# Hybrid attention and gMLP block, f32, one core: the opening runs four column blocks side by side instead of three, projection pairs change places, and four PSUM roles of the merge stage are dealt out anew

## The chip, the cores and the metric

The kernel runs on one core of one Trainium2 chip. The metric is the device time of one execution in microseconds (us). Time before: median 1210.89 us of 3 runs (1210.16 to 1210.99).

## The reference

The input x is 2048 rows of 1024 in f32. The reference computes

```python
h = _rms(x, g_pre) * (1.0 + scale) + shift          # scale, shift, gate from c @ w_ada
proj = h @ w_in                                     # 1024 -> 4864
q, k, v, z_a, u_b, v_b, z_b, g_logits = jnp.split(proj, SPLIT_IDX, axis=-1)
y_a = _swa_with_sinks(_rope(q), _rope(k), v, sinks) * silu(z_a)
y_b = gelu(u_b) * spatial_gating(layernorm(gelu(v_b))) * silu(z_b)
merged = sigmoid(g_a) * (y_a @ w_proj_a) + sigmoid(g_b) * (y_b @ w_proj_b)
out = x + gate * _rms(merged @ w_out, g_post)
```

Attention is over a window of 128 with 8 query heads and 2 key heads; the spatial gating works in chunks of 128 rows. The product h @ w_in is most of the work.

## The kernel before, in words

**Products.** A big product is done in seven products instead of eight by Winograd's form of Strassen's scheme. A *block* is 256 output columns by 1024 rows, cut into 2 by 2 quadrants ("11", "12", "21", "22": first the column half `ft`, then the row half). The seven products p = 0 to 6 use seven weight sums (A11, S1, S2, A12, S3, S4, A22) and seven sums of the activations, T[0] to T[6]. Each f32 operand is split into a high part (rounded to f32r by a cast on ACT) and a low part (the remainder, a subtraction on DVE), and `mm3` issues high x high, high x low, low x high. One block and one product are a **step**: 12 matmuls of 128x512 on TensorE (PE). In the order that `mm3` issues them, the second matmul of a step needs the low part of T, and the third the low part of W.

**Weights.** `want(n)` prepares W of step n: load, sums, high cast on ACT, low part on DVE, usually three steps ahead (LA = 3), with four W buffers. The sums of a *fresh* pair are done on DVE for the first NFIRST pairs and on GpSimd (POOL) for the later ones (`combos`). Raw loads go through SP's DMA queue and eight `raw` buffers.

**Results.** A block's products accumulate in PSUM banks with roles X, W, Y, Z (`BANK` says which product goes to which). Between products ACT copies Y<-X and Z<-Y inside PSUM, and `evac` takes the quadrants out at p = 3 ("11"), 4 ("22"), 5 ("12") and 6 ("21").

**Order.** For each half of the rows (s = 0, 1) there are 19 blocks. `slot[0]` counts steps, and `later(n, f)` places work n steps on, ahead of the step's matmuls or (post) behind them; "mid" is halfway. So the program is one fixed order on each engine, and an engine that waits holds up all that stands behind it in its queue. In the opening (s = 0) the first three blocks run product by product: p = 0 for blocks 0, 1, 2, then p = 1, and so on, 21 steps in all, with banks X/W, Y/Z and the two halves of the scores' tile S. Meanwhile T[0] to T[6] are made by `t_part` (scaling, differences and low parts on DVE, high parts on ACT). After the first product comes `second_half`: the norm of the second half of the rows (`rstd` L644, `rstd_out` L653), the other half of the conditioning matmuls (`ada_row` L681), T[1]. Then `second_rows`: `ada_fin` L693, T[2]. From step 21 on one block at a time runs in banks X, W, Y, Z. Two more banks (`bank()`, tile name b) serve small matmuls: transposes, the conditioning, attention's outputs.

**Work beside the blocks** that the change moves: the rotary embedding of k and q (`rope_finish`: `turn` loads a rotated copy, `mix` L888 multiplies on DVE and on POOL, `both` L157 adds on DVE and casts the high part on ACT L892, `low` subtracts on DVE), the layernorm steps (`ln_step`: transposes L859, statistics L863, normalization L871 on DVE), setup of the spatial gating. In the blocks of z_a each evacuation adds a multiplication on DVE (L952).

**Merge stage.** After both halves, four `Pair` blocks do both projections of one half of the rows: each step does the "a" part in banks X, Y, Z, W (`BK`) and then the "b" part in four others: two halves c[0], c[1] of the scores' tile S, and two `bank()` tiles c[2], c[3]. A step's quadrants are gated on DVE (`gated`, L1239) and added on POOL.

Of the kernel before, what the change touches and what calls it, by code (L numbers as in the profile page):

```python
# [26 lines left out]
SM = 0.125  # L27
# [23 lines left out]
NFIRST = 3  # L51
# [4 lines left out]
def hybrid_block(ctx: ExitStack, tc: tile.TileContext, xt, x, wada, wgate, wI, wP, wO,  # L56
# [488 lines left out]
    x_load(1)  # L545

# [128 lines left out]
    def ada_row(hf, kks):  # L675

        if hf not in rows:
            rows[hf] = bank()
# [10 lines left out]
    def ada_fin(hf):  # L689

        o = bank()
# [82 lines left out]
    cur["cap"] = 8  # L774
# [134 lines left out]
    def ev_kv(s):  # L909
        def ev(key, src, psum):  # L910
            h = half(key)
            if ft(key) == 0:
# [4 lines left out]
                rope_finish(h, rope_in(src, psum, "e"), put_out, (7, 4)[h] if s == 0 else h)  # L917
            else:
# [16 lines left out]
                later(2, turn, True)  # L935
# [310 lines left out]
    def run_all():  # L1246
        nonlocal T

        for s in range(NS):
            uz = [{} for _ in range(4)]  # L1250
            kinds = [lambda: ev_vb(s, 0), lambda: ev_vb(s, 2), lambda: ev_kv(s), lambda: ev_q(s, 0), lambda: ev_g(s, 0),
# [36 lines left out]
            if s == 0:  # L1288
                n0 = NFIRST
                S = pS.tile([P, 2, 512], F32, tag="s", name=nm("s"))  # L1290
                bks = [two_banks(BK["X"], BK["W"]), two_banks(BK["Y"], BK["Z"]), two_banks(S[:, 0, :], S[:, 1, :])]
                blks = [Block(bks[i], kinds[i](), "mme"[i]) for i in range(NFIRST)]
                def second_half():
                    rstd(1, BK["Z"])
                    ada_row(1, range(2))
                    rstd_out(1, BK["W"])
                    sum_to(2 * NFIRST + 2)
# [10 lines left out]
                def second_rows():  # L1308
# [231 lines left out]
```

## Time and profile before

| what | value |
|---|---|
| median of 3 runs | 1210.89 us |
| the profiled execution's own time | 1210.93 us |
| its span, first to last instruction | 1209.2 us |
| mean granted TensorE clock | 0.997 |
| PE busy | 1191.1 us, 98% of the span |
| DVE busy | 864.4 us, 71% |
| ACT busy | 631.7 us, 52% |
| POOL busy | 355.2 us, 29% |
| DMA, mean | 258 GB/s |

How to read it: the timeline has an instruction's start, its duration, engine, line, operation, what it writes and reads, and in brackets the idle time of its engine just before it with what ended that. Successive instructions of one kind are merged, "x12" is their count. The ends of matmuls are modelled and overlap the next by a little, so the length of a step is read from start to start. The stretches table gives the busy time of each engine and the count of its instructions within a piece of the span. "W<-raw,W" on DVE is the low part of a weight operand, "T<-x,AS,T" of an activation operand.

### The profile page before, as it was taken

Reading aid. Unit: us, or ns where it says so; the run is one execution under the profiler, and the core shown is the slowest. Engines: PE = TensorE matmul, PEld = TensorE weight load, DVE = VectorE, ACT = ScalarE, POOL = GpSimd, SP = SyncE. Lnnn points to the kernel's source line nnn. Section 1 sums busy time; section 2 is a strip of 40 time slices with the busy share of each in tenths; the row PEclk is TensorE's granted clock in tenths of the full one; section 3 lists DMA queues with packets and bytes.
Section 4 is the critical chain, followed back from the end, with each engine's and each line's share of the span. In section 5 each row is a group of like instructions: output and inputs, shape, how many; then the busy total and the mean of one; then the engine's idle time right before and its main releaser. Section 6 shows DMA issues by size and latency. Waiting matters only on the chain.

```text
span 1209.2 us, 17368 instructions
## 1 busy us (share of the span) xinstructions
PE 1191.1 (98%) x5450; PEld 948.9 (78%) x5450; DVE 864.4 (71%) x1315; ACT 631.7 (52%) x1367; POOL 355.2 (29%) x294
## 2 busy tenths in 40 slices
PE   9999999999999999999999999999999999999997
PEld 3567887887777777888888787777778888888886
DVE  6996889668867667358766776564886867767775
ACT  3575455576756676434345675455844512444443
POOL 0002654323366201013302222311133411155443
PEclk9999999999999999999999999999999999999999
DMA  9635997867999998578789899989967988845452
GB/s 356 225 133 190 319 336 268 253 172 199 300 348 331 315 308 295 185 222 296 259 271 284 248 259 325 280 263 294 336 213 272 383 269 267 294 150 183 131 183 87
DMA packets 227828, 311.47 MB, mean 258 GB/s; under 512 B 20884, under 2 KB 102932, under 8 KB 227736
## 3 DMA queue, kind: packets, MB, share of 16 engines
q1 hardware_dynamic: 227264, 309.68, 79.1%
q8 instruction: 43, 0.70, 0.2%
q0 software_dynamic: 176, 0.53, 0.1%
q14 instruction: 49, 0.40, 0.1%
q10 hardware_dynamic: 296, 0.16, 0.1%
HBM read 200.51 MB, written 104.53 MB: 252 GB/s over the span
## 4 chain that ended last, share of the span: by engine, by line
PE 89%; DVE 7%; ACT 2%; issue 1%; POOL 0%; DVEq 0%; ACTq 0%; POOLq 0%
PE bankY L168 28%; PE bankX L168 20%; PE bankW L168 12%; PE bankZ L168 12%; PE s L168 4%; PE b L168 3%; PE b L1091 2%; PE s L1041 2%; PE s L1042 1%; DVE W L151 1%; PE b L980 1%; DVE e L157 1%; PE b L1076 1%; DVE T L743 1%; PE b L681 1%
## 5 line engine op out<-in xcount | busy, mean ns | idle before, releaser
L168 PE MATMUL bankY<-T,W 128*128 128x512 f32 x1614 | 392.1, 392 | 0.8 <-ACT bankZ L432 0.6
L168 PEld LDWEIGHTS bankY<-T,W 128*128 128x128 f32 x1614 | 300.7, 188 | 63.7 <-ACT bankZ L432 1.0
L151 DVE TENSOR_TENSOR W<-raw,W 128x512 fp32r<-128x512 f32 x330 | 271.6, 827 | 70.6 <-ACT W L216 70.4
L168 PE MATMUL bankX<-T,W 128*128 128x512 f32 x1134 | 279.1, 394 | 1.8 <-DVE T L743 1.7
L216 ACT CAST W<-raw 128x512 fp32r<-128x512 f32 x330 | 203.7, 618 | 131.5 <-PE b L168 29.8
L168 PEld LDWEIGHTS bankX<-T,W 128*128 128x128 f32 x1134 | 210.1, 188 | 48.2 <-DVE T L743 5.0
L168 PE MATMUL bankW<-T,W 128*128 128x512 f32 x696 | 173.1, 395 | 3.4 <-DVE T L743 2.5
L168 PE MATMUL bankZ<-T,W 128*128 128x512 f32 x696 | 168.7, 391 | 0.0
L168 PEld LDWEIGHTS bankW<-T,W 128*128 128x128 f32 x696 | 128.2, 188 | 35.1 <-DVE T L743 4.7
L168 PEld LDWEIGHTS bankZ<-T,W 128*128 128x128 f32 x696 | 130.0, 188 | 26.8
L154 POOL TENSOR_TENSOR S<-x,x 128x512 f32<-128x512 f32 x28 | 37.8, 1354 | 243.0 <-DMA x<-yb 102.7
L154 POOL TENSOR_TENSOR raw<-raw,raw 128x512 f32<-128x512 f32 x48 | 76.5, 1593 | 98.8 <-DVE W L151 47.0
L154 POOL TENSOR_TENSOR S<-raw,raw 128x512 f32<-128x512 f32 x24 | 37.8, 1575 | 134.3 <-DMA raw<-in_wI 53.6
L151 DVE TENSOR_TENSOR T<-x,T 128x512 fp32r<-128x512 f32 (+1 forms) x105 | 69.6, 708 | 8.5 <-ACT T L384 8.3
L157 DVE TENSOR_TENSOR e<-bankY,e 128x512 f32<-128x512 f32 x44 | 30.4, 690 | 61.1 <-PE bankY L168 61.0
L168 PE MATMUL s<-T,W 128*128 128x512 f32 x282 | 69.4, 390 | 1.4 <-DVE q L1239 1.4
L168 PEld LDWEIGHTS s<-T,W 128*128 128x128 f32 x282 | 52.8, 188 | 12.7 <-DVE q L1239 1.8
L154 POOL TENSOR_TENSOR raw<-S,raw 128x512 f32<-128x512 f32 x24 | 34.9, 1455 | 81.8 <-DVE W L151 73.9
L384 ACT CAST T<-x 128x512 fp32r<-128x512 f32 x100 | 56.0, 619 | 2.3 <-PE s L168 2.1
L1070 ACT ACTIVATE P<-P,rc 128x128 f32<-128x128 f32 x128 | 44.5, 396 | 12.6 <-DVE rc L1066 12.3
L411 ACT COPY e<-bankW 128x512 f32<-128x512 f32 x41 | 24.0, 584 | 45.3 <-PE bankW L168 42.7
L432 ACT COPY bankZ<-bankY 128x512 f32<-128x512 f32 x42 | 24.0, 571 | 44.6 <-PE bankY L168 44.5
(267 smaller groups left out, 1453.8 us busy)
## 6 DMA issues: line engine op xcount, KB each, us to landing
raw<-in_wI SPq DMA_DIRECT2D x128, 256.0 KB, 4.6
raw<-sS SPq DMA_DIRECT2D x92, 256.0 KB, 5.0
g<-e SPq DMA_DIRECT2D x64, 256.0 KB, 4.0
sS<-raw SPq DMA_DIRECT2D x45, 256.0 KB, 4.0
T<-in_wada SPq DMA_DIRECT2D x16, 512.0 KB, 8.3
q<-q SPq DMA_DIRECT2D x64, 128.0 KB, 5.7
q<-k_s SPq DMA_DIRECT2D x64, 128.0 KB, 5.1
raw<-m SPq DMA_DIRECT2D x32, 256.0 KB, 4.5
```

The costliest lines, as they stand in the source:

```text
L151: dve.tensor_tensor(out=o, in0=a, in1=b, op=ALU.subtract)
L154: pool.tensor_tensor(out=o, in0=a, in1=b, op=op)
L157: dve.tensor_tensor(out=o, in0=a, in1=b, op=ALU.add)
L168: pe.matmul(o, w[:, i, sl], t[:, j, kt, :], start=start and kt == kts[0] and n == 0, stop=stop and kt == last and n == 2, skip_group_check ...
L216: act.copy(w[:, 0, :], src)
L384: act.copy(T[p][:, 0, kt, :], rs[kt])
L411: act.copy(self.wsb, b["W"])
L432: act.copy(self.b[to], self.b[of])
L681: pe.matmul(rows[hf][64 * i : 64 * (i + 1), :], cact[:, kk : kk + 1].broadcast_to([P, 64]), adaw[hf][kk // 4][:, kk % 4, i * 512 : (i + 1) ...
L1041: pe.matmul(o, q[:, g, :], k[:, 0, :], start=True, stop=False)
L1070: act.activation(out=st["P", kv][:, g, 0:P], in_=st["P", kv][:, g, 0:P], func=AF.Copy, scale=st["rc", kv][:, g : g + 1])
L1091: pe.matmul(o[own, :], v[:, k, own], st["pv", kv][k], start=k == 1, stop=k == 0)
```

## The change

NFIRST goes from 3 to 4: the opening runs four blocks product by product, 28 steps. The fourth block lives in the two `bank()` banks; its Y/W bank is also the bank of `ada_row(1)` and `ada_fin(1)`, and no other small matmul has a bank until step 28. The fourth block's weight sums move from POOL to DVE. `rstd(1)` stays behind step 2, but the rest of `second_half` moves behind step 3.

The pair of the first gates (`ev_g(s, 0)`) trades places with the first q pair: gates are now block 3, q blocks 4 and 5, for both halves; the weights' columns are laid out to match. What used small banks or loads in the opening is moved: the rotary work of k, the transposes of v, `setup_sgu` (19 to 24), `zero_heads` (22 to 28), `load_rope` (18 to 23), and the layernorm steps of the first half, from every three steps (22 + 3i) to five in two (27 + 5i // 2).

In the merge stage c[0], c[1] (the tile S) were X and Y of the "b" part and are now X and W; the two `bank()` tiles were Z and W and are now Y and Z.

```diff
-NFIRST = 3
+NFIRST = 4
...
-        plan = [(0, "A11", "raw"), (1, "A21", "raw"), (1, "A22", ("P", "P", "S")[n] if first else "raw"),
+        plan = [(0, "A11", "raw"), (1, "A21", "raw"), (1, "A22", ("P", "P", "x", "x")[n] if first else "raw"),
...
-                rope_finish(h, rope_in(src, psum, "e"), put_out, (7, 4)[h] if s == 0 else h)
+                rope_finish(h, rope_in(src, psum, "e"), put_out, (9, 3)[h] if s == 0 else h)
...
-                later(2, turn, True)
+                later((3, 10)[h] if s == 0 else 2, turn, True)
...
-            kinds = [lambda: ev_vb(s, 0), lambda: ev_vb(s, 2), lambda: ev_kv(s), lambda: ev_q(s, 0), lambda: ev_g(s, 0),
+            kinds = [lambda: ev_vb(s, 0), lambda: ev_vb(s, 2), lambda: ev_kv(s), lambda: ev_g(s, 0), lambda: ev_q(s, 0),
...
-                later((22, 17)[s] + 3 * i, lambda i=i: ln_step(s, i))
+                later((27 + 5 * i // 2, 17 + 3 * i)[s], lambda i=i: ln_step(s, i))
...
-                bks = [two_banks(BK["X"], BK["W"]), two_banks(BK["Y"], BK["Z"]), two_banks(S[:, 0, :], S[:, 1, :])]
-                blks = [Block(bks[i], kinds[i](), "mme"[i]) for i in range(NFIRST)]
+                bX = bank()
+                rows["bank"] = bank()
+                bks = [two_banks(BK["X"], BK["W"]), two_banks(BK["Y"], BK["Z"]), two_banks(S[:, 0, :], S[:, 1, :]),
+                       two_banks(bX, rows["bank"])]
+                blks = [Block(bks[i], kinds[i](), "mmee"[i]) for i in range(NFIRST)]
...
-                later(2, second_half, True)
-                later(3, fetch_all, True)
-                later(3, second_rows, "mid")
+                later(NFIRST - 2, lambda: rstd(1, BK["Z"]), True)
+                later(NFIRST - 1, second_half, True)
+                later(NFIRST, fetch_all, True)
+                later(NFIRST, second_rows, "mid")
...
-                    for i, (n, post) in enumerate(((-3, True), (-3, True), (-2, False), (-2, True), (-1, False), (-1, True))):
-                        later(3 * p + n, lambda p=p, i=i: t_part(p, i), post)
+                    for i, (n, post) in enumerate(((-4, True), (-3, False), (-3, True), (-2, False), (-2, True), (-1, False))):
+                        later(NFIRST * p + n, lambda p=p, i=i: t_part(p, i), post)
...
-            blk = Pair(n, (BK, {"X": c[0], "Y": c[1], "Z": c[2], "W": c[3]}))
+            blk = Pair(n, (BK, {"X": c[0], "W": c[1], "Y": c[2], "Z": c[3]}))
```

Three places show how the instructions move. The first is DVE's queue ahead of the third product (p = 2) of the opening. T_698 and T_717 are the operand T[2], x and rg, wT, Tt the rows that it is made from; W_693, W_720 are the weights of this product's first two blocks before, W_736 and W_766 now. Before:

```order
L151 TENSOR_TENSOR W_693<-P_523,W_693 128x512
L670 SCALAR_TENSOR_TENSOR x_349<-x_349,AS,e_622 128x512
L151 TENSOR_TENSOR rg<-x_348,rg 128x512
L743 SCALAR_TENSOR_TENSOR T_698<-rg,AS,T_698 128x512
L670 SCALAR_TENSOR_TENSOR x_350<-x_350,AS,e_622 128x512
L151 TENSOR_TENSOR wT<-x_349,wT 128x512
L743 SCALAR_TENSOR_TENSOR T_698<-rg,AS,T_698 128x512
L151 TENSOR_TENSOR Tt<-x_350,Tt 128x512
L743 SCALAR_TENSOR_TENSOR T_698<-wT,AS,T_698 128x512
L743 SCALAR_TENSOR_TENSOR T_698<-Tt,AS,T_698 128x512
L151 TENSOR_TENSOR W_720<-P_527,W_720 128x512
```

And now:

```order
L745 SCALAR_TENSOR_TENSOR T_717<-rg,AS,T_717 128x512
L151 TENSOR_TENSOR P_525<-S_646,raw_371 128x512
L672 SCALAR_TENSOR_TENSOR x_350<-x_350,AS,e_644 128x512
L151 TENSOR_TENSOR wT<-x_349,wT 128x512
L745 SCALAR_TENSOR_TENSOR T_717<-rg,AS,T_717 128x512
L151 TENSOR_TENSOR Tt<-x_350,Tt 128x512
L745 SCALAR_TENSOR_TENSOR T_717<-wT,AS,T_717 128x512
L745 SCALAR_TENSOR_TENSOR T_717<-Tt,AS,T_717 128x512
L151 TENSOR_TENSOR W_736<-P_525,W_736 128x512
L151 TENSOR_TENSOR P_529<-S_648,raw_373 128x512
L151 TENSOR_TENSOR W_766<-P_529,W_766 128x512
```

The sum S2 of the first block (P_525) moved in between the parts of T[2], and the low part of the first block's W stands behind all four low parts of T[2] instead of ahead of them.

The second place is DVE's queue in the middle of the first half, from the low part of step 41's weights to that of step 43's. L863 / L867 and the line behind them are the layernorm statistics, L871 / L875 its normalization, L888 / L892 is `mix`, "<-bankY" and "<-bankZ" are evacuations. Before:

```order
L151 TENSOR_TENSOR W_1633<-raw_1338,W_1633 128x512
L863 BN_STATS bst_1666<-b_1653 128x6
L864 BN_AGGR mv_1667<-bst_1666 128x2
L157 TENSOR_TENSOR e_1689<-bankY,e_1603 128x512
L151 TENSOR_TENSOR W_1662<-raw_1518,W_1662 128x512
L871 TENSOR_SCALAR q_1700<-b_1653,mv_1667,rv_1668 128x512
L157 TENSOR_TENSOR e_1603<-bankZ,e_1603 128x512
L151 TENSOR_TENSOR W_1692<-S_1659,W_1692 128x512
```

And now:

```order
L151 TENSOR_TENSOR W_1591<-raw_1287,W_1591 128x512
L151 TENSOR_TENSOR x_1395<-x_1395,x_1422 128x512
L867 BN_STATS bst_1630<-b_1616 128x6
L868 BN_AGGR mv_1631<-bst_1630 128x2
L157 TENSOR_TENSOR e_1654<-bankY,e_1552 128x512
L157 TENSOR_TENSOR e_1437<-e_1437,x_1485 128x512
L151 TENSOR_TENSOR W_1625<-raw_1471,W_1625 128x512
L892 TENSOR_TENSOR e_1335<-e_1335,m_1165 128x512
L875 TENSOR_SCALAR q_1669<-b_1616,mv_1631,rv_1632 128x512
L157 TENSOR_TENSOR e_1552<-bankZ,e_1552 128x512
L151 TENSOR_TENSOR W_1659<-S_1622,W_1659 128x512
```

The rotary work of the first q pair (here x_1395 `low`, e_1437 `both`, e_1335 `mix`), which was done several steps earlier, now shares these steps with the evacuations of the second q pair and the layernorm: eight operations between three low parts where there were five, the small aggregations included.

The third place is PE's queue in the merge stage, from the last product of the first Pair to the second product of the second. s is the tile S, b the two small banks. Before:

```order
L168 MATMUL s_8886<-T_8896,W_8970 128x512 x6
L168 MATMUL bankX<-T_8493,W_8995 128x512 x6
L168 MATMUL s_8886<-T_8493,W_8995 128x512 x6
L168 MATMUL bankW<-T_8577,W_9022 128x512 x6
L168 MATMUL b_8888<-T_8577,W_9022 128x512 x6
```

And now:

```order
L168 MATMUL b_8889<-T_8898,W_8972 128x512 x6
L168 MATMUL bankX<-T_8495,W_8997 128x512 x6
L168 MATMUL s_8888<-T_8495,W_8997 128x512 x6
L168 MATMUL bankW<-T_8579,W_9024 128x512 x6
L168 MATMUL s_8888<-T_8579,W_9024 128x512 x6
```

The last product of the first Pair no longer writes the tile S, and the first two products of the second Pair now both write it.

More of the change, by code (lines that the diff above doesn't have):

```diff
@@ L545, in hybrid_block @@
     x_load(1)
+    cur["cap"] = NFIRST - 1
+    fetch_to(NFIRST - 1)
     def rope_steps():
@@ L677, in ada_row @@
         if hf not in rows:
-            rows[hf] = bank()
+            rows[hf] = rows.get("bank") or bank()
         for kk in kks:
@@ L689, in ada_fin @@
     def ada_fin(hf):
-        o = bank()
+        o = rows.get("bank") or bank()
         for kt in range(4):
@@ L786, in hybrid_block @@
         squares(1, range(i + 2, i + 3), False)
+    want(NFIRST - 1)
     square_sums(1)
+    low_now()
     rope_do(26)
@@ L1256, in run_all @@
             if s == 0:
-                later(19, setup_sgu)
-                later(22, zero_heads)
-            later((18, 12)[s], lambda s=s: load_rope(s))
+                later(24, setup_sgu)
+                later(28, zero_heads)
+            later((23, 12)[s], lambda s=s: load_rope(s))
             for i in range(8):
-                later((22, 17)[s] + 3 * i, lambda i=i: ln_step(s, i))
+                later((27 + 5 * i // 2, 17 + 3 * i)[s], lambda i=i: ln_step(s, i))
             for c in range(4):
@@ L1317, in fetch_all @@
                     cur["cap"] = 1 << 30
-                later(2, second_half, True)
-                later(3, fetch_all, True)
-                later(3, second_rows, "mid")
-                later(3, lambda: sp.dma_start(mcpt, mcp))
-                later(3, lambda: sp.dma_start(snk8, sinks.broadcast_to([P, 8])))
-                later(9, lambda: dve.tensor_scalar(out=snk8, in0=snk8, scalar1=1.0 / SM, scalar2=None, op0=ALU.mult))
+                later(NFIRST - 2, lambda: rstd(1, BK["Z"]), True)
+                later(NFIRST - 1, second_half, True)
+                later(NFIRST, fetch_all, True)
+                later(NFIRST, second_rows, "mid")
+                later(NFIRST, lambda: sp.dma_start(mcpt, mcp))
+                later(NFIRST, lambda: sp.dma_start(snk8, sinks.broadcast_to([P, 8])))
+                later(12, lambda: dve.tensor_scalar(out=snk8, in0=snk8, scalar1=1.0 / SM, scalar2=None, op0=ALU.mult))
                 for i in range(2, 6):
-                    later(3 + (i > 2), lambda i=i: t_part(2, i), i != 3)
+                    later(NFIRST + (i > 2), lambda i=i: t_part(2, i), i != 3)
                 for p in range(3, 7):
-                    for i, (n, post) in enumerate(((-3, True), (-3, True), (-2, False), (-2, True), (-1, False), (-1, True))):
-                        later(3 * p + n, lambda p=p, i=i: t_part(p, i), post)
+                    for i, (n, post) in enumerate(((-4, True), (-3, False), (-3, True), (-2, False), (-2, True), (-1, False))):
+                        later(NFIRST * p + n, lambda p=p, i=i: t_part(p, i), post)
                 for p in range(7):
```

9 lines of the change are left out of this document (4 added, 5 removed).

## Prediction

> **What bounds the kernel now.** First the page: PE is busy for nearly the whole span, so only places where PE waits can give time back.
>
> ```profile
> span 1209.2 us, 17368 instructions
> PE 1191.1 (98%) x5450; PEld 948.9 (78%) x5450; DVE 864.4 (71%) x1315; ACT 631.7 (52%) x1367; POOL 355.2 (29%) x294
> ```
>
> The waits of PE lie in three places that the change touches: the opening, the stretch around 200 us, and the merge stage at 907 us. The table of stretches shows them by PE's busy time, and beside it how full DVE is (columns: length, then busy us and count of PE, PEld, DVE, ACT, POOL):
>
> ```profile
> 60.60:109.00 48.40, 44.87 (x186) 33.35 (x185) 42.40 (x65) 31.66 (x53) 4.32 (x3) 1.00 0.39 132
> 129.80:153.00 23.20, 23.20 (x110) 19.21 (x109) 22.18 (x29) 11.47 (x22) 16.21 (x14) 1.00 0.93 319
> 153.00:179.00 26.00, 26.00 (x123) 21.56 (x122) 22.01 (x30) 13.43 (x28) 13.81 (x14) 1.00 0.98 337
> 179.00:205.50 26.50, 25.66 (x114) 20.38 (x113) 23.93 (x31) 14.08 (x30) 14.29 (x12) 1.00 0.77 273
> ```
>
> Then PE's timeline of the opening. Each product's first step has a longer distance to the next than the others: it waits for the low parts of T or W.
>
> ```profile
> 41.59 1.94 PE L681 MATMUL b<-T,cact 128*64 128x512 f32 x8
> 44.00 1.16 PE L653 MATMUL bankW<-cst,rs 128*128 128x128 f32 x8 [0.47 <-POOL rs L148]
> ...
> 57.87 2.88 PE L168 MATMUL s<-T,W 128*128 128x512 f32 x12
> 60.59 1.07 PE L168 MATMUL bankW<-T,W 128*128 128x512 f32 x4
> ...
> 65.53 2.92 PE L168 MATMUL bankZ<-T,W 128*128 128x512 f32 x12
> ...
> 71.01 2.08 PE L168 MATMUL bankX<-T,W 128*128 128x512 f32 x7
> ...
> 74.66 2.92 PE L168 MATMUL bankY<-T,W 128*128 128x512 f32 x12
> ...
> 80.13 2.34 PE L168 MATMUL bankW<-T,W 128*128 128x512 f32 x7
> ...
> 85.08 2.92 PE L168 MATMUL bankZ<-T,W 128*128 128x512 f32 x12
> ...
> 90.55 2.43 PE L168 MATMUL bankX<-T,W 128*128 128x512 f32 x10
> ...
> 93.98 2.93 PE L168 MATMUL bankY<-T,W 128*128 128x512 f32 x12
> ...
> 99.96 2.72 PE L168 MATMUL bankW<-T,W 128*128 128x512 f32 x10
> ...
> 103.47 2.91 PE L168 MATMUL bankZ<-T,W 128*128 128x512 f32 x12
> ```
>
> A full step takes 60.59 - 57.87 = 2.72 us. The first steps of products 2 to 6 take 65.53 - 60.59 = 4.94, 3.65, 4.95, 3.43 and 3.51. Less 2.72 each, that is 2.22 + 0.93 + 2.23 + 0.71 + 0.79 = 6.9 us lost, and 0.47 for the norm before product 1.
>
> **The opening with four blocks.** A product now gives PE 4 x 2.72 = 10.9 us of work instead of 8.2. In products 2 to 6 DVE was busy 42.4 us against 5 x 8.2 = 41 us of PE's work, so it set the pace. The fourth block adds to DVE five low parts of W, three sums (S2, S3, S4; S1 falls earlier) and two additions of evacuations. An operation is priced by these rows of DVE's timeline:
>
> ```profile
> 41.77 1.29 DVE L157 TENSOR_TENSOR S<-raw,P 128x512 f32<-128x512 f32 x2
> 43.12 0.69 DVE L157 TENSOR_TENSOR S<-raw,S 128x512 f32<-128x512 f32 x1
> 45.86 1.41 DVE L670 SCALAR_TENSOR_TENSOR q<-q,AS,e 128x512 f32<-128x512 f32 x2 [0.84 <-ACT e L656]
> ...
> 64.16 0.75 DVE L743 SCALAR_TENSOR_TENSOR T<-Tt,AS,T 128x512 fp32r<-128x512 f32 x1 [0.57 <-ACT T L736]
> 64.83 0.68 DVE L151 TENSOR_TENSOR W<-P,W 128x512 fp32r<-128x512 f32 x1
> ```
>
> One alone takes 0.69 and a second behind it adds 1.29 - 0.69 = 0.60 us. Ten more make 42.4 + 6.0 = 48.4 us, against 54.4 us of PE's work: from product 3 on DVE is ahead, and those four waits go (4.7 us). The 0.47 us wait goes too: step 3 stands between the norm and its result, and POOL finishes under it.
>
> Product 2 keeps its wait. PE reaches it at 60.59 + 2 x 2.72 (the fourth steps of products 0 and 1) - 0.47 = 65.6. On DVE the chain that ends in T[2] starts with the scaling at 45.86, which waits for the norm from PE. PE now issues one step of 2.72 and then the same 1.94 us of conditioning ahead of the norm's second part, which so begins at 41.59 + 2.72 + 1.9 = 46.2 instead of 44.00: the chain starts 2.2 later, at 48.1. It ran to 64.83, 19.0 us, and now holds two operations more (S1 of the fourth block, S2 of the first): it ends at 48.1 + 19.0 + 1.2 = 68.3, and only then comes the low part of the first block's W, to 68.9. PE needs that for its third matmul, due at 65.6 + 0.45. It loses 2.8 us instead of 2.2. Products 0 and 1 keep their shape, shifted. Sum of the opening: 6.9 + 0.5 - 2.8 = **4.6 us gained**. Bounds: 2.4 if products 3 to 6 keep half of their 4.7 (DVE's slack of 6 us is a mean, and the low parts of T[3] and T[6] stand behind evacuation adds), 6.8 if product 2's wait shrinks to 0.6.
>
> The fourth block's A11 passes ahead of the second conditioning load on SP: 0.26 MB, 1.0 us at the page's mean of 258 GB/s, against a use that is 2.7 us later. All eight raw buffers are now full until the sums S3 release them, so the loads of A22 queue on SP behind the stores of products 3 and 4. Their use is two products off, 21.8 us; they cost nothing, and would show on PE only if the queue slipped by all of that. The transposes of v, the setup's matmul and the first layernorm transposes move from the opening to steps 28 and on; PE pays for them there as here, and the two rotary tables' loads keep their place right behind the fourth product's stores.
>
> **The middle.** Between 190 and 206 us PE waits for ACT's copies between banks, and ACT for a rotary sum of DVE:
>
> ```profile
> 192.99 2.88 PE L168 MATMUL bankW<-T,W 128*128 128x512 f32 x12
> 196.14 3.13 PE L168 MATMUL bankY<-T,W 128*128 128x512 f32 x12 [0.26 <-ACT bankY L432]
> 199.11 2.88 PE L168 MATMUL bankX<-T,W 128*128 128x512 f32 x12
> 202.57 3.04 PE L168 MATMUL bankY<-T,W 128*128 128x512 f32 x12 [0.58 <-ACT bankZ L432]
> 205.45 2.88 PE L168 MATMUL bankZ<-T,W 128*128 128x512 f32 x12
> ```
>
> ```profile
> 200.90 0.62 ACT L892 CAST x<-x 128x512 fp32r<-128x512 f32 x1 [3.78 <-DVE x L157]
> ```
>
> From 192.99 to 205.45 four steps take 12.46 instead of 10.9: 1.6 us lost, with DVE late and the bank copy queued behind the cast on ACT. The change pushes the rotary work of the first q pair seven steps on, into steps 36 to 45. By the orders, DVE has 22 large operations there in nine steps beside the low parts, where it had 13; in the six steps that follow, 21 instead of 19. Those nine steps are about 153 to 179 us: DVE is busy 22.0 us, less 0.09 for the overlap of each of 30 rows is 19.3 of 26. Nine more make 19.3 + 5.5 = 24.8. Four more POOL multiplications come with them, and these rows, one on DVE and one on POOL, show what one does to a DVE operation that it meets:
>
> ```profile
> 194.94 1.70 DVE L151 TENSOR_TENSOR W<-raw,W 128x512 fp32r<-128x512 f32 x1
> ```
>
> ```profile
> 194.81 1.28 POOL L154 TENSOR_TENSOR x<-x,m 128x512 f32<-128x512 f32 x1
> ```
>
> 1.70 instead of 0.69, so between 0 and 1.0 us each; I take 0.5, as not every one meets such an operation: 2.0, in all 26.8 of 26. DVE enters the stretch where PE waits already 0.8 us behind, and has two operations more there, 1.2. So **2.0 us are lost** beside the 1.6 of now. Bounds: none, if the steps up to 45 absorb it (DVE's waits there are partly its place in the queue behind PE's results); 4.5, with 1.0 us for each POOL operation and half a microsecond at the copies of the two blocks before.
>
> **The merge stage.** The second Pair's first "b" matmul waits for the DVE gating that reads the other half of the tile S:
>
> ```profile
> 904.24 1.52 PE L168 MATMUL bankX<-T,W 128*128 128x512 f32 x6
> 907.15 1.66 PE L168 MATMUL s<-T,W 128*128 128x512 f32 x6 [1.39 <-DVE q L1239]
> 908.64 1.52 PE L168 MATMUL bankW<-T,W 128*128 128x512 f32 x6
> ```
>
> ```profile
> 908.30 1.14 ACT L216 CAST W<-raw 128x512 fp32r<-128x512 f32 x2 [7.61 <-POOL raw L154]
> ...
> 909.86 0.54 ACT L493 COPY s<-s 128x512 f32<-128x512 f32 x1
> ```
>
> The step takes 908.64 - 904.24 = 4.40 instead of 2.72, 1.7 us lost. With X and W in S this wait goes, as the last reader of S is then long done. But the tile is guarded as a whole: the next step's "b" part writes W, in S, and must let ACT's copy of X out of S finish first. That copy stands on ACT behind a cast that waits for POOL until 908.30, and ends at 909.86 + 0.54 = 910.4. PE would be there at 904.24 + 2.72 + 1.36 = 908.3: it waits 2.1 us. So 1.7 goes and 2.1 comes, **0.4 us lost**; from 1.7 gained (the copy comes early) to 0.4 lost.
>
> **Sum.** -4.6 + 2.0 + 0.4 = -2.2 us on the profiled execution's 1210.93; the median of the runs is 0.04 lower, so 1210.89 - 2.2 = **1208.7 us**. A measurement of this kernel can tell about 0.2%, 2.4 us, from no change: faster means below 1208.5, slower above 1213.3. The forecast lies just inside "no change"; its own range, 1208.5 to 1211.0, is a middle that loses 2.0 to 4.5.
>
> **Rivals.**
> - *The middle absorbs the rotary work.* For it: DVE is idle 6.7 us net in the nine steps, and the 23 us before them passed with PE full though DVE was fuller there (22.18 of 23.2). Against it: PE already waits just behind. Then -4.6 + 0.4: 1206.7. Chance 0.34.
> - *The merge wait goes as well.* The two halves of S are two banks, and if POOL's sum at 908 comes 2 us earlier against PE, the copy is out in time: 1.7 gained, not 0.4 lost. With the forecast's middle 1206.6, with an absorbed middle 1204.8. Chance 0.10. [...]
> - *The opening does not do it.* Products 3 to 6 keep half of their waits: -2.4 + 2.0 + 0.4, 1210.9. Chance 0.05.
> - *Each POOL operation stops DVE for its whole length.* The four would then cost 4 x 1.28 = 5.1 us instead of 2.0, and the sum is -4.6 + 5.1 + 0.4 = 0.9 us slower, 1211.8. For it: the row of 1.70. Against it: 30 DVE rows from 153 to 179 us average 22.0 / 30 = 0.73 beside 13.8 us of busy POOL. Chance 0.04. [...]
> - *Slower: ACT's copies become late in every block.* Each rotary sum is followed on ACT by a cast, and bank copies queue behind it. If DVE lags more than about 2.7 us, one step, at the four copies of steps 42, 44, 49 and 51, PE loses up to 2.2 at each (the longest loss to DVE in this profile, product 2), 8.8 instead of 2.0 in the middle: -4.6 + 8.8 + 0.4 = 4.6 us slower, 1215.5. It decides from 6.6 us in the middle (1213.3). For it: DVE at 26.8 of 26. Against it: only two of these copies are late now. Chance 0.10.
>
> **How the numbers follow.** The forecast has 0.37; with the opening that fails and the stopped DVE, "no change" has 0.37 + 0.05 + 0.04 = 0.46. Faster: 0.34 + 0.10 = 0.44. Slower: 0.10. The range takes in the first two rivals down to 1205.6 and half of the bounds above, to 1212.2.
>
> **What would show it.** In the profile after: four blocks per product with gaps only at products 0, 1 and 2, the one at product 2 ended by DVE's W L151 (right), or gaps at 3 to 6 (wrong); DVE near full from 145 to 200 us and PE's waits for ACT's bank copies there 3 to 4 us in sum (right) or under 2 (first rival); in the merge stage no wait on q L1239, but one of about 2 us on ACT's copy, a step later (right), or none (second rival). A time under 1205 or over 1213 would say that a term is missing.

## The result, and the profile after

The changed kernel takes 1220.63 us (median of 4 runs, 1219.9 to 1221.57), the kernel before 1210.53 us beside it (4 runs, 1209.77 to 1210.99): a ratio of 1.0085, 95% interval 1.0067 to 1.0102. It is 10 us slower; the prediction was 2.2 us faster, with a range that ended at 1212.2. The profiled execution took 1221.22 us. Its page:

```profile
span 1219.5 us, 17353 instructions
PE 1191.7 (98%) x5450; PEld 951.1 (78%) x5450; DVE 866.4 (71%) x1319; ACT 631.9 (52%) x1367; POOL 345.4 (28%) x290
```

The busy times hardly moved; the lost time is PE's idle time and matmuls that last longer. To find it, both profiles are read by steps: the starts of PE's steps, each twelve big matmuls, numbered as `slot` numbers them (in the merge stage a step has two parts of six). The table gives the length of a stage, from the start of its first step to the start of the next stage, for the kernel before, the changed one, and two kernels of the experiments below.

| stage (steps) | before, us | after, us | after less before | e1_sgu | e7_all |
|---|---|---|---|---|---|
| up to step 0 | 29.96 | 29.02 | -0.94 | 30.04 | 28.67 |
| opening, 0 to 28 | 99.87 | 96.49 | -3.38 | 94.81 | 93.60 |
| behind the opening, 28 to 32 | 11.34 | 19.42 | +8.08 | 13.09 | 13.09 |
| 32 to 54 | 64.28 | 67.10 | +2.82 | 67.07 | 67.09 |
| second half, 180 to 182 | 5.44 | 6.48 | +1.04 | 6.49 | 6.48 |
| merge stage, second part of 272 to 277 | 13.92 | 16.08 | +2.16 | 14.48 | 12.71 |
| all else, to the end of the span | 984.42 | 984.92 | +0.50 | 984.90 | 984.50 |

The start is not the change's doing: in the fourteen traces of this study step 0 begins between 28.67 and 30.42 us, and e7_all and e8_cast, which are the same up to there, have 28.67 and 30.38. It is a part of the spread between runs.

The changed kernel's **opening**, in PE's timeline (start, duration, engine, line, operation, in brackets the idle time before and what ended it); step 8 is the first of product 2:

```profile
61.95 2.88 PE L168 MATMUL b<-T,W 128*128 128x512 f32 x12
64.67 0.61 PE L168 MATMUL bankW<-T,W 128*128 128x512 f32 x2
68.16 3.50 PE L168 MATMUL bankW<-T,W 128*128 128x512 f32 x10 [2.88 <-DVE W L151]
71.47 3.62 PE L168 MATMUL bankZ<-T,W 128*128 128x512 f32 x12
74.92 2.88 PE L168 MATMUL s<-T,W 128*128 128x512 f32 x12
```

As foretold, PE does two matmuls of product 2 and then waits 2.88 us for the low part of the first block's W. But the ten matmuls behind the wait take 71.47 - 68.16 = 3.31 us instead of 2.27, and the next step 3.45 instead of 2.72. Nothing in these rows waits; the matmuls themselves are slow.

**Behind the opening** there is a wait that the prediction did not have. Before, the second transposition of v (L927), the set-up's matmul (L816) and the next transposition stood two steps apart from each other, and PE waited at none:

```profile
114.38 0.60 PE L927 MATMUL b<-cst,e 128*128 128x128 f32 x4
...
120.29 1.02 PE L816 MATMUL b<-wT,ones 128*128 128x512 f32 x2
...
126.63 0.60 PE L859 MATMUL b<-cst,q 128*128 128x128 f32 x4
```

Now:

```profile
128.23 0.60 PE L931 MATMUL b<-cst,e 128*128 128x128 f32 x4
128.59 3.02 PE L168 MATMUL bankW<-T,W 128*128 128x512 f32 x12
131.45 1.02 PE L820 MATMUL b<-wT,ones 128*128 128x512 f32 x2
137.03 0.63 PE L931 MATMUL b<-cst,e 128*128 128x128 f32 x4 [4.56 <-DVE Tt L825]
137.41 4.58 PE L168 MATMUL bankY<-T,W 128*128 128x512 f32 x12
141.83 2.91 PE L168 MATMUL bankX<-T,W 128*128 128x512 f32 x12
```

L820 is the set-up's matmul (`go`), L931 the transposition of v. The second transposition follows `go` directly in PE's queue, and what ends its wait is DVE's reading of `go`'s result (`fin`, L825). So of the two small banks its tile was given the one that `go` had just written. DVE's timeline shows what stands ahead of that:

```profile
130.01 0.69 DVE L151 TENSOR_TENSOR W<-raw,W 128x512 fp32r<-128x512 f32 x1 [7.85 <-ACT W L216]
...
132.42 1.75 DVE L151 TENSOR_TENSOR W<-raw,W 128x512 fp32r<-128x512 f32 x1
134.10 1.75 DVE L892 TENSOR_TENSOR e<-e,m 128x512 f32<-128x512 f32 x1
135.77 1.11 DVE L825 SCALAR_TENSOR_TENSOR Tt<-b,col,Tt 128x128 f32<-128x128 f32 x4
```

DVE itself starts late, at 130.01, since it waited 7.85 us for ACT's cast; and ACT stood still before that cast:

```profile
128.87 0.59 ACT L926 COPY e<-s 128x512 f32<-128x512 f32 x1 [6.26 <-PE b L931]
```

This copy of v needs one of the six e buffers, and one comes free only when the first transposition (128.23) has read its e: the chain runs from PE over ACT and DVE back to PE. Step 30, from 137.41, takes 4.42 us instead of 2.72: slow matmuls again.

**The middle** has the waits that were foretold, and one more for a sum of DVE (L157):

```profile
192.40 2.99 PE L168 MATMUL bankY<-T,W 128*128 128x512 f32 x12 [0.79 <-DVE e L157]
...
202.88 3.01 PE L168 MATMUL bankY<-T,W 128*128 128x512 f32 x12 [1.59 <-ACT bankY L432]
...
209.16 3.03 PE L168 MATMUL bankY<-T,W 128*128 128x512 f32 x12 [0.55 <-ACT bankZ L432]
```

In **the second half**, at the same place of its order, stands a wait that before had none:

```profile
611.88 3.00 PE L168 MATMUL bankY<-T,W 128*128 128x512 f32 x12 [0.77 <-DVE e L157]
```

In **the merge stage** the wait for the gating is gone, and the one for ACT's copy of X is there, a step later, 1.94 us long, as worked out (2.1):

```profile
913.46 1.52 PE L168 MATMUL s<-T,W 128*128 128x512 f32 x6
914.82 1.52 PE L168 MATMUL bankW<-T,W 128*128 128x512 f32 x6
918.28 1.97 PE L168 MATMUL s<-T,W 128*128 128x512 f32 x6 [1.94 <-ACT b L493]
920.04 2.76 PE L168 MATMUL bankY<-T,W 128*128 128x512 f32 x6
922.61 1.66 PE L168 MATMUL b<-T,W 128*128 128x512 f32 x6
```

Again slow matmuls follow: the six from 920.04 take 2.57 us instead of 1.36. The table of stretches shows what the three places have in common (the granted clock is the number behind POOL's):

```profile
64.00:68.00 4.00, 1.28 (x6) 0.74 (x4) 3.43 (x6) 2.40 (x4) 0.00 (x0) 1.00 0.21 66
68.00:72.00 4.00, 3.84 (x12) 3.04 (x13) 2.63 (x6) 2.92 (x6) 0.00 (x0) 0.69 0.41 135
...
136.00:140.00 4.00, 2.97 (x11) 2.49 (x12) 3.81 (x7) 0.59 (x1) 2.58 (x2) 0.72 0.99 273
...
920.00:924.00 4.00, 4.00 (x13) 3.17 (x12) 1.13 (x2) 1.67 (x3) 0.00 (x0) 0.64 0.94 336
```

The clock that PE is granted falls from 1.00 to 0.64 to 0.72 in the 4 us around PE's return, and in this trace each of the waits of 1.9 to 4.6 us costs 1.6 to 1.7 us beyond its length.

### The profile page after: what moved, and what is told of

Its sections match the earlier page's. It is cut to its first block, busy times and chain, and to the rows that moved or that the text cites. A ratio compares the mean times of both kernels' runs of the same rounds, so it can differ in the third digit from the quotient of the medians.

```text
span 1219.5 us, 17353 instructions
## 1 busy us (share of the span) xinstructions
PE 1191.7 (98%) x5450; PEld 951.1 (78%) x5450; DVE 866.4 (71%) x1319; ACT 631.9 (52%) x1367; POOL 345.4 (28%) x290
## 4 chain that ended last, share of the span: by engine, by line
PE 89%; DVE 6%; ACT 2%; issue 2%; POOL 1%; DMA 0%; SPq 0%; DVEq 0%; POOLq 0%; ACTq 0%
PE bankY L168 28%; PE bankX L168 19%; PE bankZ L168 12%; PE bankW L168 12%; PE b L168 4%; PE s L168 4%; PE b L1095 2%; PE s L1045 2%; PE s L1046 1%; PE b L984 1%; DVE W L151 1%; PE b L1080 1%; PE b L683 1%; DVE e L157 1%; PE b L863 0%
## 5 line engine op out<-in xcount | busy, mean ns | idle before, releaser
L168 PE MATMUL bankY<-T,W 128*128 128x512 f32 x1578 | 386.1, 393 | 3.7 <-ACT bankY L432 1.6
L168 PEld LDWEIGHTS bankY<-T,W 128*128 128x128 f32 x1578 | 295.6, 189 | 66.2 <-issue 2.3
L168 PE MATMUL bankX<-T,W 128*128 128x512 f32 x1110 | 272.5, 393 | 1.0 <-DVE T L745 1.0
L168 PEld LDWEIGHTS bankX<-T,W 128*128 128x128 f32 x1110 | 205.8, 188 | 45.4 <-DVE T L745 3.0
L168 PE MATMUL bankW<-T,W 128*128 128x512 f32 x684 | 169.9, 395 | 4.6 <-DVE W L151 2.9
L168 PE MATMUL bankZ<-T,W 128*128 128x512 f32 x684 | 166.4, 392 | 0.0
L168 PEld LDWEIGHTS bankW<-T,W 128*128 128x128 f32 x684 | 126.7, 189 | 34.4 <-DVE T L151 3.4
L168 PEld LDWEIGHTS bankZ<-T,W 128*128 128x128 f32 x684 | 128.4, 189 | 26.6
L154 POOL TENSOR_TENSOR raw<-raw,raw 128x512 f32<-128x512 f32 x46 | 73.2, 1590 | 92.5 <-DVE W L151 31.4
L157 DVE TENSOR_TENSOR e<-bankY,e 128x512 f32<-128x512 f32 x43 | 29.6, 689 | 59.3 <-PE bankY L168 59.0
L168 PE MATMUL b<-T,W 128*128 128x512 f32 x270 | 66.4, 390 | 0.0
L168 PE MATMUL s<-T,W 128*128 128x512 f32 x258 | 63.5, 391 | 1.9 <-ACT b L493 1.9
L168 PEld LDWEIGHTS b<-T,W 128*128 128x128 f32 x270 | 50.9, 189 | 10.6
L168 PEld LDWEIGHTS s<-T,W 128*128 128x128 f32 x258 | 48.4, 188 | 12.4 <-ACT b L493 2.4
```

What stands on the lines that cost most here:

```text
L154: pool.tensor_tensor(out=o, in0=a, in1=b, op=op)
L157: dve.tensor_tensor(out=o, in0=a, in1=b, op=ALU.add)
L168: pe.matmul(o, w[:, i, sl], t[:, j, kt, :], start=start and kt == kts[0] and n == 0, stop=stop and kt == last and n == 2, skip_group_check ...
```

## The experiments

Theory: the 10 us are (a) the wait for the shared small bank, (b) slow matmuls behind three long waits, (c) the reordered pairs, in both halves, against an opening that gains some 3 us. Rivals: DVE and ACT are late as a whole, so that waits only move when one is removed; and the slow matmuls have nothing to do with the waits. Times are medians, beside the kernel before in the same series on the same chip.

| kernel | us (runs) | before, us | ratio, 95% interval |
|---|---|---|---|
| e1_sgu | 1212.91 (12) | 1211.02 | 1.0021 (1.0012 to 1.0030) |
| e2_roles | 1218.30 (5) | 1211.02 | 1.0064 (1.0052 to 1.0076) |
| e4_p2 | 1219.67 (5) | 1211.02 | 1.0071 (1.0059 to 1.0083) |
| e5_pairs | 1214.71 (6) | 1211.02 | 1.0032 (1.0020 to 1.0044) |
| e6_xz | 1211.10 (11) | 1211.34 | 0.9997 (0.9988 to 1.0006) |
| e7_all | 1208.46 (11) | 1211.34 | 0.9980 (0.9971 to 0.9989) |
| e8_cast | 1208.89 (11) | 1211.34 | 0.9982 (0.9973 to 0.9991) |
| e9_after | 1219.99 (5) | 1211.34 | 1.0078 (1.0066 to 1.0091) |
| e10_fill | 1219.77 (5) | 1211.40 | 1.0068 (1.0055 to 1.0082) |
| e11_noln | 1206.19 (5) | 1211.40 | 0.9961 (0.9949 to 0.9974) |
| e12_role1 | 1210.24 (11) | 1211.40 | 0.9991 (0.9982 to 1.0000) |
| e13_act | 1210.69 (11) | 1211.58 | 0.9997 (0.9988 to 1.0006) |

### e1_sgu: the set-up one step later

```diff
-                later(24, setup_sgu)
+                later(25, setup_sgu)
```

> The changed kernel (1220.6 us), with the set-up of the causal table one step later, so that its matmul stands behind the second transposition of v on PE and the two take different small banks. Theory: PE's 4.6 us wait for DVE's four operations on that matmul goes, and with it the slow matmuls behind it (1.7 us): 6 to 7.5 us faster, about 1213.5 us. Rival: DVE and ACT are late there anyway, because ACT stood still for 6.3 us for an e buffer just before, so PE waits for them a step or two later instead: above 1217 us.

1212.91 us, 7.7 us less than the changed kernel at its first measurement (7.1 less than at its second, e9_after). The stage behind the opening takes 13.09 us instead of 19.42, and PE's waits of over 0.1 us there are gone:

```profile
130.79 0.60 PE L931 MATMUL b<-cst,e 128*128 128x128 f32 x4
131.14 2.99 PE L168 MATMUL bankY<-T,W 128*128 128x512 f32 x12
133.97 1.02 PE L820 MATMUL b<-wT,ones 128*128 128x512 f32 x2
```

ACT's standstill is still there, 6.26 us in this trace too. The theory holds: what PE paid for was the bank, and the late DVE only set how long. Of the 6.33 us, 4.56 were the wait and 1.63 the slow matmuls (nine of them, each start to start less 0.227). The 1.75 us that the stage still takes over before are for the larger part (1.2 us) the small matmuls that left the opening.

This kernel's trace also holds the two other long waits, and there they were followed by matmuls at full speed:

```profile
65.69 0.61 PE L168 MATMUL bankW<-T,W 128*128 128x512 f32 x2
69.19 2.56 PE L168 MATMUL bankW<-T,W 128*128 128x512 f32 x10 [2.88 <-DVE W L151]
71.59 2.88 PE L168 MATMUL bankZ<-T,W 128*128 128x512 f32 x12
```

Ten matmuls in 2.40 us behind a wait as long as the one of the changed kernel. So the opening is 94.81 us here and 96.49 there, a difference of 1.68. The kernel's 12 runs fit this: eight took 1211.6 to 1213.5 us at a mean granted clock of 0.997 or 0.998, the other four 1213.2 to 1217.6 at 0.992 to 0.996.

### e2_roles: the old roles in the merge stage

```diff
-            blk = Pair(n, (BK, {"X": c[0], "W": c[1], "Y": c[2], "Z": c[3]}))
+            blk = Pair(n, (BK, {"X": c[0], "Y": c[1], "Z": c[2], "W": c[3]}))
```

> The changed kernel, with only the roles of the scores' banks in the merge stage as they were before (X and Y in the tile of the scores). Theory: the 1.94 us wait for ACT's copy and the slow matmuls behind it (1.7 us) go, the old wait of 1.4 us comes back: 2.2 us faster, about 1218.4 us. Rival: ACT and POOL are late there because of what comes before, whatever the roles; then a wait of 2 us stays and the time is within 0.7 us of 1220.6.

1218.30 us: 1.7 to 2.3 us faster than the changed kernel, as the theory has it. The old wait is back, and no slow matmuls follow it; the merge stage takes 13.91 us in this trace instead of 16.08:

```profile
914.26 1.65 PE L168 MATMUL s<-T,W 128*128 128x512 f32 x6 [1.38 <-DVE q L1243]
```

In this trace the 2.88 us wait at product 2 is there too, and no slow matmuls follow that one either.

### e4_p2: product 2's low part of W earlier

```diff
-                    later(NFIRST + (i > 2), lambda i=i: t_part(2, i), i != 3)
+                    later(NFIRST + (i > 2), lambda i=i: (i == 4 and low_now(), t_part(2, i)), i != 3)
```

> The changed kernel, with the low part of the first block's W of product 2 put on DVE two low parts of T earlier. Theory: product 2's one wait of 2.9 us breaks into waits of under 1 us for the low parts of T, as before the change, and no slow matmuls follow: 2.5 to 3.5 us faster, about 1217.5 us. Rival: the chain on DVE as a whole is what is late, so that the wait only moves behind another low part: under 1 us faster.

1219.67 us, between 0.3 and 1.0 us faster (by the ratios to before 0.8 to 1.7). In the trace the wait of 2.88 is one of 0.29 and one of 0.52:

```profile
65.56 2.88 PE L168 MATMUL bankW<-T,W 128*128 128x512 f32 x10 [0.29 <-DVE W L151]
68.96 3.31 PE L168 MATMUL bankZ<-T,W 128*128 128x512 f32 x12 [0.52 <-ACT W L216]
```

and smaller ones between single matmuls: steps 8 and 9 still take 4.31 and 3.15 us, together 2.0 more than two full steps. No slow matmuls follow: the next step takes 74.83 - 72.11 = 2.72 us. Its opening takes 122.66 - 28.98 = 93.68 us, 1.1 less than e1_sgu's, where the same wait had no slow matmuls, and 2.8 less than the changed kernel's. The trace is on the side of the theory; the median, with no more than 1.0 us (1.7 by the ratio), is nearer to the rival's. All five runs were at 0.993 or 0.994, and the trace has slow matmuls behind the two other long waits. The pair e6_xz and e7_all, which differ by this edit alone, decides.

### e5_pairs: the kernel before, with the pairs reordered alone

```diff
-            kinds = [lambda: ev_vb(s, 0), lambda: ev_vb(s, 2), lambda: ev_kv(s), lambda: ev_q(s, 0), lambda: ev_g(s, 0),
+            kinds = [lambda: ev_vb(s, 0), lambda: ev_vb(s, 2), lambda: ev_kv(s), lambda: ev_g(s, 0), lambda: ev_q(s, 0),
...
-    cols = [wvb, wk, wv, wq[:, 0:256]] + gates(0) + [wq[:, 256:512], wza]
+    cols = [wvb, wk, wv] + gates(0) + [wq, wza]
```

> The kernel before (1210.5 us), with only the pairs reordered: the gate pair ahead of the first q pair, in the weights' columns and in the evacuations. Theory: the two rotary pairs behind each other are what costs 2.7 us in the middle and 1.0 us at 612 us: 2 to 3.7 us slower, about 1213.5 us. Rival: the middle loses because the layernorm steps and rotary slots moved with the opening; then only the 1.0 us of the second half comes, 1211.5 us.

1214.71 us, 3.7 us slower than before: the full price of the theory. From step 42 to 54 it takes 37.66 us, before 35.27, +2.39; from 180 to 182 it is +1.05, behind a wait of 0.76 us for DVE's L157. The changed kernel takes 37.99 us from 42 to 54, so the moved layernorm steps and rotary slots add 0.3 us at most.

### e6_xz: X and Z in the tile of the scores

```diff
-            blk = Pair(n, (BK, {"X": c[0], "W": c[1], "Y": c[2], "Z": c[3]}))
+            blk = Pair(n, (BK, {"X": c[0], "Z": c[1], "Y": c[2], "W": c[3]}))
```

> The kernel of e1_sgu (1212.9 us), with X and Z of the second Pair's b part in the tile of the scores in place of X and W. Theory: W's first product no longer has to let ACT's copy of X out of that tile finish, so PE's wait of 1.93 us goes, and with it the slow matmuls that follow it in some runs; the wait of 1.4 us of before doesn't return, since Z and X are read early: about 1210.8 us. Rival: the guard of the whole tile only moves the wait, to the product that writes X right after ACT's copy into Z: 1212 us or more.

1211.10 us; by the ratios to before 2.9 us faster than e1_sgu. The merge stage takes 12.71 us, before 13.92, e1_sgu 14.48. Both waits are gone; a wait of 0.17 us for ACT's copy of Y is left.

### e7_all: all three edits

The changed kernel with the edits of e1_sgu, e4_p2 and e6_xz.

> The kernel of e6_xz with the earlier low part of e4_p2 as well. Theory: product 2's wait goes from 2.9 to under 1 us, which e4's trace puts at 1.2 us behind equal starts, and no idle time of PE above 1.6 us is left, so no run has slow matmuls behind one: about 1209.5 us, all runs within 1.5 us and at a granted clock of 0.996 or more. Rival: the slow matmuls don't hang on the idle times; then runs at 0.992 to 0.994 remain and the times spread over 3 us or more.

1208.46 us, a ratio of 0.9980 (0.9971 to 0.9989): **faster than both kernels**, by 2.9 us than before. It is 2.6 us below e6_xz (2.1 by the ratios), in whose trace the wait of 2.90 us at product 2 was followed by nine slow matmuls: the edit of e4_p2 is worth what its trace showed. The 11 runs lie between 1207.84 and 1210.15 us, at 0.997 to 0.999: a spread of 2.3 us where 1.5 was expected, but no run at a low clock, where its neighbours e1_sgu and e6_xz had them from 0.992 and 0.995 on. PE's waits, with the sum, the count and the longest (us):

```profile
PE bankW L168 <- DVE T L151: 1.7, 3, 0.7
PE bankY L168 <- ACT bankY L432: 1.6, 1, 1.6
PE bankY L168 <- DVE e L157: 1.5, 2, 0.8
```

None that is left behind the opening is longer than 1.6 us. The opening takes 93.60 us, as in e4_p2.

### e8_cast: the rotary's cast one step later

```diff
         def both():
             add(R, R, st["rot"])
+
+        def cast():
             act.copy(st["hi"], R)
...
         later(6 + wait, both, True)
+        later(7 + wait, cast, True)
```

> The kernel of e7_all, with ACT's cast of each rotary result issued one step later. Theory: in the middle PE waits 1.6 and 0.55 us for bank copies that stand on ACT behind a cast that waits for DVE's sum; a cast that comes when the sum is long done holds nothing up: 1.5 to 2 us faster than e7_all. Rival: DVE itself is what is late there, and the wait turns up behind another of its operations: within 0.5 us of e7_all.

1208.89 us: the same as e7_all within the intervals, so the rival. In the trace the wait of 0.55 us is gone and that of 1.6 is 1.43. The two places that the edit was made for are shorter, steps 32 to 54 by 0.4 us and 180 to 182 by 0.8, but 1.0 us more is spent elsewhere, 0.4 of it right behind the second place. So ACT's queue was a small part; that DVE is what is late is tried in e11_noln.

### e9_after: the changed kernel again

> The changed kernel again, unedited. Theory: PE's three long idle times (2.9, 4.6 and 1.9 us) are each followed by some ten slow matmuls, 1.7 us, in some runs and not in others, as e1_sgu's trace shows idle times of 2.88 and 1.93 us without them: times in a band of up to 5 us below 1221.5, the lower the higher the mean granted clock, about 1.7 us for 0.0014 of it. Rival: slow matmuls follow every idle time of this kernel: all runs within 1 us of 1220.6, at 0.993 to 0.994.

Five runs, 1219.23 to 1222.85 us, at 0.991 to 0.994: three of them within the rival's band, two above both; nearer to the rival as far as this kernel goes. In the trace the three waits (2.85, 4.56, 1.94 us) are again all followed by slow matmuls. Two runs at 0.991 and 0.992 were 3 us slower still; no trace of such a run exists.

### e10_fill: the wait of the merge stage filled with work

```diff
             for ab in range(2):
+                if self.n == 1 and p == 1 and ab == 1:
+                    for _ in range(9):
+                        pe.matmul(self.b[1]["Z"], w[:, 0, 0:P], T[p][:, 0, 0, :], start=True, stop=True, skip_group_check=True)
                 mm3(self.b[ab][BANK[p]], w, T[p], (2 * ab, 2 * ab + 1), FRESH[p], True)
```

> The changed kernel, with nine matmuls of no use (2.04 us, into the free bank of Z) on PE ahead of the product that waits 1.94 us for ACT in the second Pair. The wait is then filled with work and as long as before. Theory: the ten slow matmuls behind it come from PE's idle time and go: the step to the next b product is 1.7 us shorter, the granted clock there stays 1.0, and the kernel is about 1.6 us faster than 1220.3. Rival: the clock falls there for another reason (what the other engines or DMA do at 916 us); then the matmuls stay slow, the fill adds 0.1 us, and the time is unchanged.

PE's timeline there (L458 are the nine matmuls):

```profile
916.45 2.20 PE L458 MATMUL b<-T,W 128*128 128x512 f32 x9
918.55 1.66 PE L168 MATMUL s<-T,W 128*128 128x512 f32 x6
920.04 1.52 PE L168 MATMUL bankY<-T,W 128*128 128x512 f32 x6
921.40 1.52 PE L168 MATMUL b<-T,W 128*128 128x512 f32 x6
```

and its stretches:

```profile
916.00:920.00 4.00, 4.00 (x18) 3.11 (x17) 2.64 (x3) 3.15 (x6) 2.71 (x3) 1.00 0.73 229
920.00:924.00 4.00, 4.00 (x19) 3.30 (x19) 1.42 (x2) 2.71 (x5) 0.18 (x1) 1.00 0.98 354
```

PE goes on with the Pair's second step no earlier than it did, but the clock stays at 1.00, the six matmuls from 920.04 take 1.36 us, and the stage takes 925.48 - 911.01 = 14.47 us instead of 16.08: 1.61 us gained by work of no use. In the 4 us of the wait POOL and ACT do what they do in the changed kernel (2.71 us against 2.60, 3.15 against 3.14), and DMA is as full; only PE's idle time is different. The trace is on the side of the theory. It is one trace, though, and of the four traces in which this wait stood unfilled one, e1_sgu's, had no slow matmuls either; what speaks for the theory besides is gathered in the last section. The median, 1219.77, is 0.2 to 0.9 us below the changed kernel's two (1.2 to 2.1 by the ratios), less than the 1.6 of the trace, and does not decide.

### e11_noln: three layernorm steps left out in the middle

```diff
-        later(5, stats)
-        later(6, norm)
+        if s == 0 and i > 4:
+            later(6, lambda: store(1, vn_s[s][:, i, :], t.rearrange("p a b -> p (a b)")))
+        else:
+            later(5, stats)
+            later(6, norm)
```

> The kernel of e7_all (1208.5 us), without the statistics and the normalization of the last three layernorm steps of the first half (three large and three small DVE operations, 5 us in steps 44 to 50; the raw values are stored in place of the normalized ones). Theory: the 2.9 us that PE loses between 182 and 200 us come from DVE, which has more work there than PE: they go for the larger part, 2 to 2.9 us faster. Rival: they come from the chain of each rotary result (POOL, DVE, ACT's cast, ACT's bank copy), however much else DVE does: under 1 us faster.

1206.19 us; by the ratios to before 2.3 us faster than e7_all. Both waits for ACT's bank copies are gone, though nothing of ACT's was changed; one for DVE is left:

```profile
183.78 3.01 PE L168 MATMUL bankY<-T,W 128*128 128x512 f32 x12 [1.69 <-DVE e L157]
```

So DVE is what is late. But the amount of its work is not all: from step 32 to 54 this kernel takes 65.30 us, 1.8 less than e7_all and still 1.0 more than the kernel before, which did the three steps that are left out here. The order of DVE's work has its part.

### e12_role1: the kernel before, with X and Z in the tile

The edit of e6_xz, on the kernel before.

> The kernel before (1211.2 us), with only the scores' banks of the second Pair in other roles: X and Z in their tile. Theory: the 1.39 us wait for DVE's gating goes and none comes in its place: 1.4 to 1.7 us faster, about 1209.6 us. Rival: PE's wait there is given back at the next wait for ACT or POOL, whose operations come no earlier: within 0.5 us of before.

1210.24 us, 0.9991 (0.9982 to 1.0000), 1.2 us faster by the medians. The trace has the merge stage at 12.72 us, 1.2 less than before: 1.55 gained at the wait, 0.35 given back two parts later, where 0.17 us of waiting for ACT's copy of Y come up. So it lies nearer to the theory, a little short of its figure.

### e13_act: the last four normalizations on ACT

```diff
             pow_rstd(rv, mv[:, 1:2], 1.0)
+            if s == 0 and i > 3:
+                st["nb"] = small(1, "pw")
+                pool.tensor_scalar(out=st["nb"], in0=mv[:, 0:1], scalar1=rv, scalar2=-1.0, op0=ALU.mult, op1=ALU.mult)
...
+            if s == 0 and i > 3:
+                act.activation(out=vn, in_=st["b"], func=AF.Identity, scale=rv, bias=st["nb"])
+            else:
+                dve.tensor_scalar(out=vn, in0=st["b"], scalar1=mv[:, 0:1], scalar2=rv, op0=ALU.subtract, op1=ALU.mult)
```

> The kernel of e7_all (1208.5 us), with the normalization of the last four layernorm steps of the first half on ACT in place of DVE (four operations of 0.8 us leave DVE; ACT is half idle there). Theory: DVE is what is late between 182 and 200 us, so that most of 4 x 0.7 = 2.8 us of work less there shows: 1 to 2 us faster, about 1207 us. Rival: ACT's queue, in which the bank copies stand, gets as much later as DVE gets earlier: within 0.5 us of e7_all.

1210.69 us: 2.2 us slower than e7_all, worse than the rival. In PE's timeline the wait for ACT's bank copy has grown from 1.6 to 2.82 us, and slow matmuls follow it:

```profile
194.75 4.44 PE L168 MATMUL bankY<-T,W 128*128 128x512 f32 x12 [2.82 <-ACT bankY L432]
```

The step takes 198.99 - 194.75 = 4.24 us instead of the 2.85 that the same step takes in e7_all. The wait for DVE's L157 has shrunk from 0.8 to 0.5. What ACT does ahead of that copy counts, even where it is half idle.

## Why the prediction was wrong

**The step that failed** is this one: "The transposes of v, the setup's matmul and the first layernorm transposes move from the opening to steps 28 and on; PE pays for them there as here". They were priced by their own length, and not by what stands between them: the second transposition of v got the bank of the set-up's matmul, directly behind it on PE, and with the bank a wait for DVE. It cost 6.3 us in the trace (4.6 of waiting, 1.6 of slow matmuls) and 7.1 to 7.7 us by the medians. e1_sgu undid it alone.

**A term that was missing** are the slow matmuls behind long waits. Each wait was priced at its length; the three long ones of the changed kernel cost 1.68 (product 2, the changed kernel's opening against e1_sgu's), 1.63 (behind the opening) and 1.61 us more (merge stage, against e10_fill): 4.9 us. The longest wait in the profile of before that was quoted was 1.39 us, and no slow matmuls followed it; the price could not be read there, but waits of 2.8 and 2.1 us were foretold and nothing bounded what lay past the longest row. The prediction's own sign for a missing term, a time over 1213, came true.

The terms one by one:

- *Opening, -4.6.* Without slow matmuls it is 94.81 - 99.87 = -5.1 us (e1_sgu), of which 1.75 us (the excess of the steps behind it, mostly small matmuls) only moved: -3.3. Product 2 loses 5.90 - 2.72 = 3.2 us there against the 2.8 of the prediction, at the very low part that it named; products 3, 4 and 5 lose nothing, as foretold. Product 6 loses 4.30 - 2.72 = 1.6 us, where it was to lose nothing and had lost 0.8 before: in the changed kernel's trace two DVE operations ahead of T[6]'s parts take 1.79 and 1.78 us, not 0.69, beside two POOL sums (1.73 and 1.62 us), which "from product 3 on DVE is ahead", a statement on the mean of five products, did not see. The prediction's lower bound had T[6]'s low parts in it, for another reason. With product 2 mended (e7_all) the opening is 93.60 us, and -4.5 is left of the change: the size that was forecast, reached with an edit.
- *Middle, +2.0.* Measured +2.8; e5_pairs puts +2.4 of it on the order of the pairs alone, and e11_noln shows DVE to be what is late. The first rival, that the middle absorbs it, is refuted. That its size came near is in part luck, as the rows below show.
- *Second half, nothing.* Measured +1.0, and +1.05 in e5_pairs. The new order holds for both halves, and the prediction priced it in the first alone.
- *Merge stage, +0.4.* The wait went and the new one came where they were put, at 1.94 us instead of 2.1. Without slow matmuls the stage is +0.55 (e1_sgu); with them +2.16.

On the middle: DVE was to be overfull in steps 36 to 45 (26.8 of 26 us), with two operations more in the steps behind them. In the changed kernel's trace it is busy 23.3 of 26.4 us in steps 36 to 45, and in steps 45 to 54 it runs 39 operations instead of 31. It is nearly full only from some 174 us on (DVE is the third busy time):

```profile
148.00:174.00 26.00, 26.00 (x123) 21.52 (x122) 22.30 (x30) 11.53 (x25) 16.59 (x15) 1.00 0.88 291
174.00:200.00 26.00, 25.21 (x119) 20.56 (x118) 25.45 (x35) 12.31 (x25) 17.07 (x15) 1.00 0.89 307
```

PE's waits for ACT's bank copies came to 2.1 us, between the 3 to 4 that were named as the forecast's sign and the first rival's "under 2"; 0.8 us of waiting for DVE itself stands beside them.

The sum of the profiled execution: -3.3 (opening), +4.7 (behind it, 8.08 - 1.75 - 1.63), +4.9 (slow matmuls), +2.8, +1.0, +0.55 (merge stage), +0.5 (all else, of which no place is above 0.4), -0.9 (the start): +10.25, where the spans differ by 10.28. That is 12.45 more than the forecast's -2.2: 4.7 and 4.9 for the two steps above, 1.0 for the second half, 1.3 too little gained in the opening, 0.8 in the middle, 0.15 in the merge stage and 0.5 elsewhere, less 0.9 for the start.

The slower rival of the prediction, ACT's copies late in every block, did not happen: three waits in the middle, not four of 2.2 us. The slower result came from a place that no rival named.

## What to carry to other kernels

A small operation that moves takes its buffer with it: before it is priced at its own length, look in the built program which bank or buffer it is given, who read that last, and where this reader stands in its own queue. A wait of PE of 1.9 us or more is worth breaking into short ones, since behind 13 of the 16 in these traces another 1.0 to 1.75 us was lost; filling it with matmuls of no use took 1.6 us off the stage in the one trace of it. And an order that is written once may run twice: price it at each of its places.

## What the runs showed of the hardware

**Slow matmuls behind PE's idle time.** In the fourteen traces there are 16 idle times of PE, behind the first product, of 1.9 us or more. Slow matmuls (the next starts over 0.3 us later, instead of 0.227) followed 13 of them: all five of 4.55 and 4.56 us, five of the seven of 2.82 to 2.90, three of the four of 1.93 and 1.94. After the idle times of 0.6 to 1.69 us at most three were counted. Behind the long ones 5 to 10 matmuls are slow, within 3 to 5 us, and the loss is 1.0 to 1.75 us. A sharper mark are matmuls of the products (L168) that start 0.42 to 0.43 us apart: there are 82 of them behind the first product, all of them behind these 13 idle times, and none in the six traces without an idle time of 1.9 us. The first comes 0.5 to 1.6 us behind PE's return. With one of these idle times filled with work, and the other engines and DMA about as busy, there is none at that place (e10_fill, one trace). Together this points to the idle time as the cause. The lowest granted clock of a 4 us stretch behind such an idle time is 0.50, at 136 to 140 us in e10_fill. The length of the idle time does not settle it alone: the same 2.88 us had slow matmuls in the changed kernel and none in e1_sgu, and 1.93 to 1.94 us was enough three times in four. What decides within 1.9 to 2.9 us was not tried.

**Open.** Runs at a mean granted clock of 0.991 and 0.992 (1222.85 and 1217.61 us for two kernels) lose more than their long waits explain, and the kernel before, whose trace has no long wait, has six runs at 0.994, from 1211.94 to 1213.97 us; no trace shows where. Whether the wait behind the opening would have been short had ACT not stood still for an e buffer was not tried either.
